# One FFN output product: steps of P2 among those of P5 and P6, Q4 in the transposes' PSUM banks, a tile of its own for the last P7, plane transfers on two steps

## The chip, the cores and the metric

The kernel runs on one core of one Trainium2 chip. The metric is the device time of one execution in microseconds (us), the median over several runs. Engine names: PE is TensorE, DVE is VectorE, ACT is ScalarE, POOL is GpSimd, SP is SyncE, which here only issues DMAs. PE sums into eight PSUM banks of 128 x 512 float32.

## What is computed

Two layers of a decoder trunk on 512 positions and 1024 channels, float32. Each layer is a half-weighted FFN, a token mixer and a second half-weighted FFN:

```python
def swiglu(x, w_in, w_out):                 # w_in 1024 x 5632, w_out 2816 x 1024
    g, u = jnp.split(x @ w_in, 2, axis=-1)
    return (jax.nn.silu(g) * u) @ w_out

for i in range(2):
    h = h + 0.5 * swiglu(rms_norm(h, ffn1_norm[i]), ffn1_w_in[i], ffn1_w_out[i])
    hn = rms_norm(h, mix_norm[i])
    m = recurrent_mixer(hn, ...) if i == 0 else spatial_gating_mixer(hn, ...)
    h = h + m
    h = h + 0.5 * swiglu(rms_norm(h, ffn2_norm[i]), ffn2_w_in[i], ffn2_w_out[i])
return rms_norm(h, final_norm)
```

So four FFNs, in the order FFN 1 and FFN 2 of layer 0, FFN 1 and FFN 2 of layer 1, with the recurrent mixer between the first two and the spatial one between the last two. The change concerns the output product, `(512 x 2816) @ (2816 x 1024)`, of the first three of them.

## The kernel before

**Number format.** Every float32 operand of a large product is split into a high part `hi` (rounded to the format that PE multiplies) and the rest `lo`; a product is three matmuls, hi·hi, lo·hi and hi·lo (L421, L422, L423). ACT writes `hi` (`act`, L103) and DVE `lo` (`tt`, L94). For the weights these are `whi` and `wlo`, made by `Sub.split`.

**Seven products.** A product of 2 x 2 blocks is done with seven products instead of eight (the form of Winograd). On the left stand blocks of the activations and sums of them, on the right blocks of the weights and sums of them:

```python
LEFT = {"P1": "A11", "P2": "A12", "P5": "S1", "P6": "S2", "P3": "S4", "P7": "S3", "Q4": "A22"}
```

The weight sums are made in SBUF. One raw tile (`Raw`, 128 x 1024 float32, 512 KB) holds two K blocks of 128 rows and 512 columns. SP loads it (`Raw.fetch`, L142). A further block is added to it in place by an accumulating DMA that POOL issues (`Raw.add`, L145), or DVE adds another tile to it (`Sub.add`, L94). For a cut i of the K dimension the weights go from product to product, in `seven` with `chain`:

- P1 and P2 load their own block.
- P5i loads the block (0,0) and gets (0,1) by an accumulating DMA, two steps after the load (`wait=2`).
- P6i takes P5i's tile; DVE adds the tile (1,1) to it. Right behind P6i's split POOL issues the addition of (1,0): that makes Q4i's weights.
- P3i loads (1,1). Right behind its split POOL issues the addition of (0,1): that makes P7i's weights. So P7i's tile is there only when P3i is split and the transfer that follows has landed.

**One output product per FFN.** In three FFNs (`FF_WHOLE`, `CHAIN`) the whole K of 22 blocks, 11 per half, is done in one pass: `out_blocks` calls `seven` with six cuts, cut 0 of one K block, the others of two. A step is one product over one cut, six matmuls per K block (12 in most steps). There are 7 x 6 = 42 steps, in the order that `CHAIN` spells out by hand: six of P1, six of P2, then a middle in which P5, P6 and four of Q4 alternate, then a tail with P3, P7 and the last two of Q4. The fourth FFN goes in three passes and doesn't use `CHAIN`.

**What sets the order.** The program is written out step by step into one queue per engine (the loop at the end of `trunk`): in step i the pending additions go to POOL, the hooks "pre" are run, weights are split up to `SPLIT_AHEAD = 3` steps ahead, the hooks "mid" and "rest" are run, further raw tiles are loaded while fewer than `RAW_BUFS = 8` are in use, the matmuls of step i follow, then the hooks "end" and "late". Nothing is reordered after that; each engine works through its queue and waits where data are missing. There are four buffers each for `whi` and `wlo`.

**PSUM.** Six banks in `mmp` (`bank`), two in `auxp` (`aux`). In the output product P1 sums into two banks A, P2 into B, P5 into C, and Q4, whose sums are kept apart here (`apart`), into two banks Q. P6 and later P7 continue in A, P3 in C:

```python
BANK = {"P1": ("A", True), "P2": ("B", True), "P5": ("C", True), "P6": ("A", False), "P3": ("C", False),
        "P7": ("A", False), "Q4": ("A", False)}
```

**What follows each product.** Behind the last step of P2, P3, P7 and Q4 DVE adds the sums to the quarters of the residual `X` (`upd`, L100): A11, A12, A22, A21. As each quarter is finished (`norm.quarter`) the next norm takes it up: squares on ACT, then transposes on PE by which the next block gets its left operands. Two of the norms do that in blocks (`BlockNorm`; transposes in `Group.turn`, L274, tile `e`; the splits behind them in tiles `hi` and `lo`). The first FFN's norm (`TileNorm`) scales whole rows first (`rows`, tile `xn`) and transposes these in two halves of sixteen (`turn`, L615, tile `xt`). The first two of four banks of a half are from `aux`.

**The left operands of a chained FFN** come from the input half of the FFN, in chunks of four columns of tiles (`chunk`, `left_blocks`). `Group.cross` transposes them by DMA: `move` copies the float32 halves apart into planes (tile `pl`, ACT) and issues two transposing DMAs on SP for each of two names (L320), all in one step; `merge` puts them together five and six steps later.

**Neighbours on the queues.** In the output product of the first FFN the gate weights of the recurrent mixer are fetched from step 8 on (`load_gates`: POOL clears a tile, L1105, then SP loads it, L1109, eight loads in all). In that of the third FFN ACT issues four DMAs of the spatial mixer in step 34 (`prep_ws`, L1287 and L1291). The first raw tiles of the stage behind (for an FFN, by `PairRaw`, L936) are loaded as slots come free in the tail.

Of the kernel before, what the change touches and what calls it, by code (L numbers as in the profile page):

```python
# [14 lines left out]
P = 128  # L15
# [34 lines left out]
CHAIN = ([("P1", i) for i in range(6)] + [("P2", i) for i in range(6)]  # L50
# [9 lines left out]
def trunk(ctx: ExitStack, tc: tile.TileContext, a: dict, out: bass.AP):  # L60
# [194 lines left out]
    class Group:  # L255
# [48 lines left out]
        def cross(self, half, tiles, planes, merges, parts):  # L304

            w, names = 2 * self.n * P, ("A12", "A11") if half == 0 else ("S1", "A22")
            if half == 0:
                names = names[::-1]
            dt = {}

            def move():
                pl = [sp.tile([P, 2 * T], U16, tag="s", name=nm("pl"))[:, : 2 * w] for _ in tiles]
                for k, name in enumerate(names):
                    c = slice(k * w, (k + 1) * w)
                    d = dt[name] = sp.tile([P, 2 * T], U16, tag="s", name=nm("dt"))[:, : 2 * w]
                    v = d.rearrange("p (m s t) -> p m s t", s=2, t=P)
                    for s, (t, h) in enumerate(zip(pl, tiles)):
                        act(t[:, c].rearrange("p (b f) -> p b f", b=2),
                            h.bitcast(U16)[:, c].rearrange("p (f b) -> p b f", b=2), AF.Copy)
                        nc.sync.dma_start_transpose(out=v[:, :, s, :], in_=t[:, c])  # L320
                tiles.clear()

            def merge(name):
                act(self.new(name).bitcast(U16).rearrange("p (x b) -> p x b", b=2),
                    dt.pop(name).rearrange("p (b x) -> p x b", b=2), AF.Copy)

            hook(*planes, move)
            for name, at in zip(names, merges):
                hook(*at, lambda name=name: merge(name))
            for name, at in zip(names, parts):  # L330
                hook(*at, lambda name=name: self.parts(name))
# [42 lines left out]
    def seven(block, cuts, left, w, posts, order=None, own=False, apart=False, joined=None, opening=None,  # L374
# [14 lines left out]
        def mm_of(prod, ci):  # L389
# [3 lines left out]
            def mm(sub):  # L393
                if fresh and ci == 0:
                    for s in range(2):
                        bk[name, s] = bank(name)[:, :w]
                if prod == joined and ci == 0:
                    held.extend((sub, q, i) for q, i in enumerate(pairs))
                    return
                if opening and prod == "P1":  # L400
                    qs = list(enumerate(pairs))
                    for n, (q, i, m, s) in enumerate([(q, i, m, s) for q, i in qs for m in range(3) for s in range(2)]
                                                     if ci == 0 else
                                                     [(q, i, m, s) for m in range(3) for q, i in qs for s in range(2)]):
                        if n == (4 if ci else 6):
                            opening[ci]()
                        nc.tensor.matmul(bk[name, s], left(prod, i, s)[m == 1], (sub.lo if m == 2 else sub.hi)[:, q, :],
                                         start=(i, m) == (0, 0), stop=(i, m) == (cuts[-1][-1], 2))
                    for s in range(2 * ci):
                        posts[prod](s, bk[name, s])  # L410
                    return
                for s in range(2):
                    ps = bk[name, s]
                    k = {} if fresh else dict(skip_group_check=True)
                    if prod == joined and also is not None:
                        also(s, ps)
                    for sb, q, i in (held if prod == joined else []) + [(sub, q, i) for q, i in enumerate(pairs)]:
                        zh, zl = left(prod, i, s)
                        wh, wl = sb.hi[:, q, :], sb.lo[:, q, :]
                        end = i == cuts[-1][-1]  # L420
                        nc.tensor.matmul(ps, zh, wh, start=fresh and i == 0, stop=False, **k)  # L421
                        nc.tensor.matmul(ps, zl, wh, start=False, stop=False, **k)  # L422
                        nc.tensor.matmul(ps, zh, wl, start=False, stop=end, **k)  # L423
                    if ci == len(cuts) - 1 and prod in posts:
                        posts[prod](s, ps)
# [4 lines left out]
        def far(ci):  # L430
            return own and order.index(("P6", ci)) - order.index(("P5", ci)) >= 4

        def again(ci):
            return own and order.index(("P5", ci)) - order.index(("P1", ci)) >= 6

        for prod, ci in order:
# [8 lines left out]
            if chain:  # L445
# [4 lines left out]
                elif prod == "P6":  # L450
                    r, tile, then = raw[11, ci], new(1, 1), block(1, 0, cuts[ci])
                elif prod == "P3":
                    r, then = new(1, 1), block(0, 1, cuts[ci])
                    raw[33, ci] = r
                else:
                    r = raw[33 if prod == "P7" else 11, ci]
            elif prod == "P1":
# [82 lines left out]
    class BlockNorm:  # L540


        def __init__(self, grow, plain=False, late=False, wait=()):


            self.g = [Group(2), Group(2)]
            self.grow, self.plain, self.late, self.wait = grow, plain, late, wait

        def src(self, i, name):
# [4 lines left out]
        def quarter(self, name):  # L554
# [5 lines left out]
            at = n + (2 if name == "A11" or name in self.wait else 1)  # L560
            for i, g in enumerate(self.g):
                g.stage(at, name, *self.src(i, name), self.plain if name == "A21" else name != "A22",
                        bank if self.late and name == "A11" else None,
                        direct=int(name == "A21" and not self.plain), lag=i)
            if name == "A21":
                S.z = self.g
# [22 lines left out]
    class TileNorm:  # L589
# [14 lines left out]
                    else:  # L604
                        ts(o, xt(t, c), S.rt[:, t : t + 1], None, ALU.mult)

        def turn(self):
            self.ps = []
            for j in range(4):
                ps = (aux if j < 2 else bank)("xt")  # L610
                for q in range(2):
                    c, k = divmod(2 * j + q, 4)
                    for s in range(2):
# [16 lines left out]
        def quarter(self, name):  # L630
# [18 lines left out]

# [1049 lines left out]
```

## Time and profile before

| | |
|---|---|
| runs | 1600.75, 1605.91, 1604.55 us; median 1604.55 |
| profiled execution | 1606.85 us, its span in the trace 1605.0 |
| granted PE clock, mean | 0.992 |
| PE busy, first output product (225.86 to 344.91) | 112.92 of 119.05 us |
| PE busy, second (700.87 to 815.79) | 110.47 of 114.92 us |
| PE busy, third (1029.98 to 1144.13) | 110.81 of 114.15 us |
| PE busy, rest of the kernel up to 1144.13 | without a gap |
| DVE busy in the three | 102.84, 98.50, 98.85 us |

The times in the second column count from the start of the span. A busy time says how long an engine had an instruction at work; a busy PE can still be slow, when its granted clock is below 1.00. In a row of instructions the releaser behind `<-` is what the engine waited for last, with the time of idleness before it.

### The profile page before, as it was taken

To read this page: it belongs to the slowest core of one execution; us is meant where nothing else is said; L and a number is where in the kernel's file an instruction comes from. 1 tells how busy PE (TensorE), PEld (TensorE's weight loads), DVE (VectorE), ACT (ScalarE), POOL (GpSimd) and SP (SyncE) were. 2 spreads that over 40 slices of the span, in tenths; PEclk is the share of its full clock that TensorE was granted. 3 is DMA by queue.
4 is the path that set the end of the run, shared out by engine and by line. 5 is a ranking of instruction groups with operands and counts; after the bars stand their busy time and mean duration, and the time that the engine had idled before them with its cause. 6 is when DMAs were issued, how large, how long until landed. Compare 5 with 4: busy or idle time off the path is not lost.

```text
span 1605.0 us, 20741 instructions
## 1 busy us (share of the span) xinstructions
PE 1581.6 (99%) x7149; PEld 1304.4 (81%) x7149; DVE 1315.6 (82%) x1759; ACT 1158.9 (72%) x1696; POOL 222.5 (14%) x201
## 2 busy tenths in 40 slices
PE   9999999999999999999899999999999999999998
PEld 7788887788888888888788888887788888888886
DVE  6977777978998877778878777789878989889788
ACT  7877786558777777786567777865786775675676
POOL 2111103200010111102201111022211011111120
PEclk9999999999999999999999999999999999999999
DMA  8888779953283887779937888799888557796793
GB/s 292 182 189 192 186 213 245 202 138 97 87 213 103 178 205 193 182 222 240 209 99 182 190 193 186 211 253 200 218 199 209 158 124 194 181 221 172 174 225 100
DMA packets 247465, 299.24 MB, mean 186 GB/s; under 512 B 94672, under 2 KB 120384, under 8 KB 247360
## 3 DMA queue, kind: packets, MB, share of 16 engines
q1 hardware_dynamic: 197856, 204.78, 41.4%
q0 software_dynamic: 47712, 91.30, 33.9%
q10 hardware_dynamic: 1792, 1.84, 0.3%
q8 instruction: 56, 0.92, 0.2%
q14 instruction: 49, 0.40, 0.1%
HBM read 275.84 MB, written 2.10 MB: 173 GB/s over the span
## 4 chain that ended last, share of the span: by engine, by line
PE 79%; DMA 6%; issue 5%; DVE 4%; ACT 2%; POOL 1%; ACTq 0%; SPq 0%; POOLq 0%
PE A L421 12%; PE A L422 12%; PE A L423 12%; PE C L422 6%; PE C L423 6%; PE C L421 6%; DMA raw<-in_ffn_w_out_dram 6%; PE p L892 4%; PE B L421 3%; PE B L423 3%; PE B L422 3%; PE r L232 2%; PE r L234 2%; PE r L233 2%; PE e L274 1%
## 5 line engine op out<-in xcount | busy, mean ns | idle before, releaser
L94 DVE TENSOR_TENSOR wlo<-raw,whi 128x1024 fp32r<-128x1024 f32 (+1 forms) x537 | 639.0, 1192 | 230.6 <-ACT whi L103 228.6
L103 ACT ACTIVATE whi<-raw 128x1024 fp32r<-128x1024 f32 (+1 forms) x537 | 553.1, 1031 | 237.5 <-PE C L422 58.4
L421 PE MATMUL A<-whi,hi 128*128 128x512 f32 x1016 | 401.0, 395 | 1.9 <-ACT c L103 1.9
L422 PE MATMUL A<-whi,lo 128*128 128x512 f32 x1016 | 396.9, 391 | 0.0
L423 PE MATMUL A<-wlo,hi 128*128 128x512 f32 x1016 | 396.9, 391 | 0.0
L421 PEld LDWEIGHTS A<-whi,hi 128*128 128x128 f32 x1016 | 191.9, 189 | 46.7 <-ACT c L103 7.9
L423 PEld LDWEIGHTS A<-wlo,hi 128*128 128x128 f32 x1016 | 191.4, 188 | 40.6 <-DVE wlo L94 0.4
L422 PEld LDWEIGHTS A<-whi,lo 128*128 128x128 f32 x1016 | 191.8, 189 | 39.0 <-DVE lo L94 0.3
L422 PE MATMUL C<-whi,lo 128*128 128x512 f32 x560 | 218.9, 391 | 1.3 <-DVE lo L94 1.2
L421 PE MATMUL C<-whi,hi 128*128 128x512 f32 x560 | 218.2, 390 | 0.0
L423 PE MATMUL C<-wlo,hi 128*128 128x512 f32 x560 | 218.1, 389 | 0.0
L145 POOL DMA_DIRECT2D raw<-in_ffn_w_in_dram x82 | 99.1, 1215 | 731.4 <-ACT pl L103 312.2
L103 ACT ACTIVATE hi<-a 128x512 fp32r<-128x512 f32 (+1 forms) x188 | 111.6, 600 | 55.9 <-DVE a L94 54.3
L145 POOL DMA_DIRECT2D raw<-in_ffn_w_out_dram x72 | 83.3, 1196 | 367.4 <-DVE wlo L94 185.6
L94 DVE TENSOR_TENSOR raw<-raw,raw 128x1024 f32<-128x1024 f32 (+1 forms) x108 | 129.6, 1200 | 0.9
L422 PEld LDWEIGHTS C<-whi,lo 128*128 128x128 f32 x560 | 105.1, 188 | 25.8 <-DVE lo L94 4.1
L421 PEld LDWEIGHTS C<-whi,hi 128*128 128x128 f32 x560 | 105.2, 188 | 21.9
L94 DVE TENSOR_TENSOR lo<-a,hi 128x512 fp32r<-128x512 f32 (+1 forms) x188 | 122.0, 656 | 1.3 <-ACT hi L103 1.2
L423 PEld LDWEIGHTS C<-wlo,hi 128*128 128x128 f32 x560 | 105.1, 188 | 21.6
L422 PE MATMUL B<-whi,lo 128*128 128x512 f32 x280 | 109.1, 389 | 0.1
L421 PE MATMUL B<-whi,hi 128*128 128x512 f32 x280 | 109.0, 389 | 0.0
L423 PE MATMUL B<-wlo,hi 128*128 128x512 f32 x280 | 109.0, 389 | 0.0
(184 smaller groups left out, 2081.3 us busy)
## 6 DMA issues: line engine op xcount, KB each, us to landing
raw<-in_ffn_w_in_dram SPq DMA_DIRECT2D x161, 512.0 KB, 4.3
raw<-in_ffn_w_out_dram SPq DMA_DIRECT2D x100, 512.0 KB, 5.6
raw<-in_ffn_w_in_dram POOLq DMA_DIRECT2D x82, 512.0 KB, 7.0
raw<-in_ffn_w_out_dram POOLq DMA_DIRECT2D x60, 512.0 KB, 7.5
raw<-in_sg_w_in_dram SPq DMA_DIRECT2D x20, 512.0 KB, 6.2
raw<-in_ffn_w_in_dram SPq DMA_DIRECT2D x34, 256.0 KB, 6.5
raw<-in_rec_w_in_dram SPq DMA_DIRECT2D x16, 512.0 KB, 3.7
raw<-in_sg_w_in_dram POOLq DMA_DIRECT2D x12, 512.0 KB, 7.7
```

What stands on the lines that cost most here:

```text
L94: nc.vector.tensor_tensor(out=o, in0=x, in1=y, op=op)
L103: nc.scalar.activation(out=o, in_=x, func=f, **k)
L145: nc.gpsimd.dma_start(out=self.v, in_=src, accum_op=ALU.add)
L232: nc.tensor.matmul(ps, wh, xh, start=start, stop=False)
L233: nc.tensor.matmul(ps, wh, xl, start=False, stop=False)
L234: nc.tensor.matmul(ps, wl, xh, start=False, stop=stop)
L274: nc.tensor.transpose(ps[:, o : o + P], src(q, s), ident)
L421: nc.tensor.matmul(ps, zh, wh, start=fresh and i == 0, stop=False, **k)
L422: nc.tensor.matmul(ps, zl, wh, start=False, stop=False, **k)
L423: nc.tensor.matmul(ps, zh, wl, start=False, stop=end, **k)
L892: nc.tensor.matmul(bank_of(half, s), z, (sub.lo if m == 2 else sub.hi)[:, q, :], start=left[2] == "2" and (h, q, m) == (0, 0, 0), stop=lef ...
```

## The change

It is confined to the three chained output products and to the chunks in front of them.

- `CHAIN`: P1 stays first. P2, which followed it in six steps, is put among the steps of P5, P6 and Q4, with P20 behind P50 and P25 next to the end of the middle. The tail is the same as before, from P30 to Q45.
- Banks: the two Q banks are taken from `aux` in a chained product. The norm behind it (`norm.chain`) takes banks from `mmp` for its transposes, except those of A21. For `TileNorm` the first half takes all four banks from `mmp`, the second as before two of each.
- P75: a product P7 that stands fewer than four steps behind P3 of its cut (`linked`) doesn't continue P3's tile but gets a tile of its own, block (0,1) loaded by SP and (1,1) added by POOL two steps later. In `CHAIN` that is P75 alone; P35 then has no addition behind its split. One 512 KB load more per chained FFN, as many additions as before.
- `Group.cross`: `move` is called once for each of the two names, on two successive steps; the merges stay where they were.

```diff
-CHAIN = ([("P1", i) for i in range(6)] + [("P2", i) for i in range(6)]
-         + [("P5", 0), ("P5", 1), ("P6", 0), ("P5", 2), ("P6", 1), ("P5", 3), ("P6", 2), ("Q4", 0), ("Q4", 1),
-            ("P5", 4), ("P6", 3), ("Q4", 2), ("P5", 5), ("P6", 4), ("Q4", 3), ("P6", 5)]
-         + [("P3", 0), ("P3", 1), ("P3", 2), ("P3", 3), ("P7", 0), ("P7", 1), ("P3", 4), ("P7", 2), ("P3", 5),
-            ("P7", 3), ("P7", 4), ("P7", 5), ("Q4", 4), ("Q4", 5)])
+CHAIN = [("P1", i) for i in range(6)]
+CHAIN += [(s[:2], int(s[2])) for s in
+          "P50 P20 P51 P60 P21 P52 P61 P22 P53 P62 Q40 P23 P54 P63 Q41 P24 P55 P64 Q42 P25 P65 Q43".split()]
+CHAIN += [(s[:2], int(s[2])) for s in "P30 P31 P32 P33 P70 P71 P34 P72 P35 P73 P74 P75 Q44 Q45".split()]
...
-            def move():
-                pl = [sp.tile([P, 2 * T], U16, tag="s", name=nm("pl"))[:, : 2 * w] for _ in tiles]
-                for k, name in enumerate(names):
-                    c = slice(k * w, (k + 1) * w)
...
-                tiles.clear()
+            def move(k, name):
+                if k == 0:
+                    dt["pl"] = [sp.tile([P, 2 * T], U16, tag="s", name=nm("pl"))[:, : 2 * w] for _ in tiles]
+                c = slice(k * w, (k + 1) * w)
...
-            hook(*planes, move)
+            for k, name in enumerate(names):
+                hook(planes[0] + k, planes[1], lambda k=k, name=name: move(k, name))
...
-                        bk[name, s] = bank(name)[:, :w]
+                        bk[name, s] = (aux if chain and name == "Q" else bank)(name)[:, :w]
...
+        def linked(ci):
+            return order.index(("P7", ci)) - order.index(("P3", ci)) >= 4
+
...
                 elif prod == "P3":
-                    r, then = new(1, 1), block(0, 1, cuts[ci])
-                    raw[33, ci] = r
+                    r = raw[33, ci] = new(1, 1)
+                    if linked(ci):
+                        then = block(0, 1, cuts[ci])
+                elif prod == "P7" and not linked(ci):
+                    r = new(0, 1, (1, 1))
                 else:
                     r = raw[33 if prod == "P7" else 11, ci]
...
-                        bank if self.late and name == "A11" else None,
+                        bank if (self.late and name == "A11") or (self.chain and name != "A21") else None,
...
-        def turn(self):
+        def turn(self, half):
             self.ps = []
             for j in range(4):
-                ps = (aux if j < 2 else bank)("xt")
+                ps = (aux if j < 2 and half else bank)("xt")
...
-                hook(n + 2, "end", self.turn)
+                hook(n + 2, "end", lambda: self.turn(0))
...
-                hook(n + 3, "end", self.turn)
+                hook(n + 3, "end", lambda: self.turn(1))
...
-        chain = not hasattr(norm, "last")
+        chain = norm.chain = not hasattr(norm, "last")
```

More of the change, by code (lines that the diff above doesn't have):

```diff
@@ L309, in cross @@
             dt = {}
-            def move():
-                pl = [sp.tile([P, 2 * T], U16, tag="s", name=nm("pl"))[:, : 2 * w] for _ in tiles]
-                for k, name in enumerate(names):
-                    c = slice(k * w, (k + 1) * w)
[L315 to L320, printed above, removed]
-                tiles.clear()
+            def move(k, name):
+                if k == 0:
+                    dt["pl"] = [sp.tile([P, 2 * T], U16, tag="s", name=nm("pl"))[:, : 2 * w] for _ in tiles]
+                c = slice(k * w, (k + 1) * w)
+                d = dt[name] = sp.tile([P, 2 * T], U16, tag="s", name=nm("dt"))[:, : 2 * w]
+                v = d.rearrange("p (m s t) -> p m s t", s=2, t=P)
+                for s, (t, h) in enumerate(zip(dt["pl"], tiles)):
+                    act(t[:, c].rearrange("p (b f) -> p b f", b=2),
+                        h.bitcast(U16)[:, c].rearrange("p (f b) -> p b f", b=2), AF.Copy)
+                    nc.sync.dma_start_transpose(out=v[:, :, s, :], in_=t[:, c])
             def merge(name):
@@ L546, in __init__ @@
             self.g = [Group(2), Group(2)]
+            self.chain = False
             self.grow, self.plain, self.late, self.wait = grow, plain, late, wait
```

## The prediction

> **What bounds the kernel now.** I read the page first, then the busy time by stretches, cut at step boundaries of the three output products that the change touches, then the waits of TensorE (PE), and last the chain of waits around each.
>
> ```profile
> span 1605.0 us, 20741 instructions
> PE 1581.6 (99%) x7149; PEld 1304.4 (81%) x7149; DVE 1315.6 (82%) x1759; ACT 1158.9 (72%) x1696; POOL 222.5 (14%) x201
> ```
>
> PE is the bound: 23.4 us of the span are all that it ever idles. A gain can come only out of that and out of stretches in which it runs slowly. Stretches (start and end, length, busy time and count of each engine, granted clock, DMA share, GB/s), one P1+P2 run, then three middles (P50 to the first P3 step), then three tails (to the end of Q45):
>
> ```profile
> 700.87:730.79 29.92, 29.92 (x133) 24.78 (x132) 24.34 (x35) 23.55 (x33) 4.51 (x4) 1.00 0.90 246
> 255.78:300.20 44.42, 42.13 (x175) 33.51 (x174) 37.75 (x50) 26.48 (x40) 10.88 (x12) 0.96 0.93 220
> 730.79:771.78 40.99, 40.78 (x183) 33.34 (x182) 37.43 (x48) 27.05 (x41) 10.30 (x10) 1.00 0.96 229
> 1059.90:1102.06 42.16, 41.15 (x183) 33.26 (x182) 36.79 (x49) 25.66 (x40) 10.71 (x10) 1.00 0.92 219
> 300.20:344.91 44.71, 40.87 (x174) 33.28 (x173) 41.40 (x66) 28.96 (x48) 6.49 (x6) 0.92 0.83 186
> 771.78:815.79 44.01, 39.76 (x173) 32.61 (x172) 36.73 (x49) 27.16 (x45) 6.02 (x5) 0.92 0.78 186
> 1102.06:1144.13 42.07, 39.74 (x173) 31.97 (x172) 38.52 (x50) 28.43 (x46) 10.22 (x10) 0.96 0.98 228
> ```
>
> and, from the timeline, eight transposes of the normalisation:
>
> ```profile
> 734.87 1.04 PE L274 MATMUL e<-ident,x 128*128 128x128 f32 x8
> ```
>
> P1+P2 has 132 product matmuls in 29.92 us: 0.2267 us each, and a two-block step of 12 takes 2.72. A middle has 29 K blocks of six matmuls, 174 x 0.2267 = 39.4; the second and third also hold eight transposes (1.0, last row). A tail has 26 blocks, 35.4, and sixteen transposes, 2.1. So the three middles are 5.0, 0.5 and 1.7 us too long and the three tails 7.2, 6.5 and 4.6: 25.5 us in all, the most that this change can win. Who waits in them:
>
> ```profile
> PE e L274 <- DVE x L100: 6.3, 3, 4.1
> PE xt L615 <- ACT xn L103: 3.2, 1, 3.2
> PE Q L421 <- ACT whi L103: 1.3, 1, 1.3
> ```
>
> and the longest of these in the timeline:
>
> ```profile
> 796.04 0.39 PE L423 MATMUL A<-wlo,hi 128*128 128x512 f32 x1
> 800.55 2.35 PE L274 MATMUL e<-ident,x 128*128 128x128 f32 x8 [4.12 <-DVE x L100]
> 803.12 0.63 PE L422 MATMUL A<-whi,lo 128*128 128x512 f32 x1
> 803.55 0.63 PE L423 MATMUL A<-wlo,hi 128*128 128x512 f32 x1
> ```
>
> An idle stretch is paid twice: after the 4.12 us the matmuls start 0.43 us apart (803.12, 803.55) instead of 0.2267, and the first two tails have a granted clock of 0.92. "TensorE: Matmul & The Clock Gate" in the Trainium skill (Why this matters for your kernels) says that only gaps over about 3 us do this; by that rule the 1.3 us wait in the first middle should have left the clock alone, and that middle has 0.96, so I let the row decide.
>
> **The last P7 on its own tile.** P75's weights are P35's tile plus an accumulating transfer that GpSimd (POOL) can issue only when P35 is split. The chain of waits before the 4.12 us:
>
> ```profile
> 788.53 8.34 DMA raw<-in_ffn_w_out_dram
> 796.97 1.06 ACT whi L103
> 798.06 0.56 DVE wlo L94
> ...
> 799.89 0.22 DVE x L100
> ```
>
> and the rows that P74's tile hangs on: its split on ACT, its add on POOL, the load for which the slot of P70 was used, and the median landings of SP's and POOL's transfers:
>
> ```profile
> 790.01 1.04 ACT L103 ACTIVATE whi<-raw 128x1024 fp32r<-128x1024 f32 x1
> 783.85 1.20 POOL L145 DMA_DIRECT2D raw<-in_ffn_w_out_dram  x1 [4.99 <-DVE wlo L94]
> 778.92 0.92 SPq L936 DMA_DIRECT2D raw<-in_ffn_w_in_dram  x2
> raw<-in_ffn_w_out_dram SPq DMA_DIRECT2D x100, 512.0 KB, 5.6
> raw<-in_ffn_w_out_dram POOLq DMA_DIRECT2D x60, 512.0 KB, 7.5
> ```
>
> The split waits for the transfer, and the update of x behind it, on which the transposes wait, stands in VectorE's (DVE) queue behind that split. In the changed program P75 has a tile loaded when P70 is split, with its add two steps later: the 8.34 us are gone from this chain. What is late next is P74. Its add (783.85) now stands on POOL behind P75's add, which waits for its load: that load takes the slot freed at 778.92, lands 5.6 later at 784.5, POOL needs 1.2, so P74's add goes out at 785.7, 1.9 us later, and lands by the median 7.5 at 793.2. P74's split began at 790.01: it would be 1.9 us late (if the add lands as fast as it must have) to 4.0 us (by the 8.34). Against this, that split could have begun when PE ended P34, at 788.1 (771.78 + 2 x 1.36 + 5 x 2.72), and was 1.9 us late for a backlog on DVE that the middle leaves (next part). P75's round from split to x takes 4.1 us (796.97 to about 801.1), P74's before it one step, 2.7: without any wait x would be there some 7 us after 790.0, at 797, and PE is ready for it at 796.3 (796.04 + 0.2267). With the backlog gone and P74 0 to 4.0 late on that, the idle time is 0 to 2.9 us instead of 4.12; I take 1.5, and 0.6 at half rate. The second FFN, with a tail 6.5 too long, saves 4.4.
>
> In the first FFN the normalisation of rows follows, and its root stands behind the same split:
>
> ```profile
> 319.48 7.76 DMA raw<-in_ffn_w_out_dram
> 327.34 1.07 ACT whi L103
> ...
> 332.06 1.97 PE xt L615 x8
> ```
>
> The split that waits 7.76 us for its tile ends at 328.4, and from there to the transposes are 3.6 us. The update of x is in place before it here, so without that wait the 3.2 us of PE idle shrink by 0 to 2.8, by how late P74 is; I take 2, and 1.0 of matmuls at half rate: 3.0. In the third the chain is another:
>
> ```profile
> 1122.53 1.22 ACTq L1291
> 1123.87 1.07 ACT whi L103
> 1128.70 1.29 DVE x L100 x2
> ```
>
> ScalarE (ACT) issues four DMAs of the next mixer from step P34 on, the split comes after them, x after that. The change leaves them where they are. I give it 1.0 (0 to 2, or up to 2 worse if P74 is late on top).
>
> Cost of the tile: three more 512 KB loads on SyncE's (SP) queue, and the next stage's first loads one slot later. At 246 GB/s (first stretch row) that is 2.1 us each; the steps that need the delayed tiles come eight and more steps later, so I cost it at nothing; uncovered it is 2.1 us in each.
>
> **P2 over the middle.** The same steps in another order, no matmul more. What it does to supply:
>
> ```profile
> 273.79 2.00 ACT L103 ACTIVATE whi<-raw 128x1024 fp32r<-128x1024 f32 x2 [3.54 <-DMA raw<-in_ffn_w_out_dram]
> 272.97 2.44 POOL L145 DMA_DIRECT2D raw<-in_ffn_w_out_dram  x2 [9.36 <-DMA raw<-in_ffn_w_out_dram]
> SPq L1109 <- POOL gw L1105: 8.0, 1, 8.0
> 261.89 10.52 DMA raw<-in_ffn_w_out_dram
> 1066.67 9.64 DMA raw<-in_ffn_w_out_dram
> L94 DVE TENSOR_TENSOR wlo<-raw,whi 128x1024 fp32r<-128x1024 f32 (+1 forms) x537 | 639.0, 1192 | 230.6 <-ACT whi L103 228.6
> ```
>
> All middle stalls end in a split of Q4 or P3 whose add is not there. The add for Q4 goes out when P6 is split. Before, it is needed four or five steps later (Q41: P51, P60, P52, P61, which are 9.5 us, against 9.64 in the last row). In the new order seven to nine steps lie between, for Q40 the shortest, 15.0 us. In the first FFN SP also stands still: eight gate loads wait 8.0 us for POOL's memsets, and these for the adds ahead of them (POOL waited 9.36 us for a load later on), while the weight load at the end of it lands after 10.52. In the new order two adds fewer stand ahead of the memsets, so part of this goes. DVE is busy 91% of a middle (37.43 of 40.99) and 81% of P1+P2 (24.34 of 29.92); with P2's half mixed in it comes to 49.6 of 55.9, 89%. Over the whole second product it is busy 98.5 us (the three rows) of the 107.9 that PE needs without a wait, so it is no bound of its own, but makes up a hole only over many steps. I keep 1 us of stall in the first FFN and 0.7 in the others together: of 7.2 us 5.5 are saved. What moves the other way: the x update of P2, the squares and the transposes of A11 now come after P25, at the start of the tail. That is some 2.6 us of DVE (two updates, 1.29 in the row above, and two lo like them) in a tail where it is busy 36.73 of some 37.5 us net, part of that the backlog. Splits run three steps, 8.2 us, ahead of PE, so it is covered; if the backlog stays, it costs up to 2.6 in each of two FFNs. I take 1.4 for all new costs (0 to 6).
>
> **Q4 in the transposes' banks; two plane transfers a step.** Q keeps the two spare banks from Q40 to the end, and the transposes take banks that B and C have left two or more steps earlier (B at P25, C at P35); for the first FFN four banks are needed after P74, and exactly four are free. Nothing waits. The plane transfers are split over two steps, their merges stay; the chunk stages around them run without a gap (P1+P2 row: busy 29.92 of 29.92), so there is nothing to win and five steps of cover to lose. Both zero, the second within 1 us.
>
> **Sum.** 4.4 + 3.0 + 1.0 + 5.5 - 1.4 = 12.5. The profiled execution took 1606.85 us around its span of 1605.0; the median of the runs is 1604.55, 0.14% less, which changes a saving of 12.5 us by nothing. 1604.55 - 12.5 = 1592.0. With the bounds: 20 us if P74 is on time and the middle clean, 6 if its wait is at its worst.
>
> **Rivals.**
> 1. *P74 takes over P75's wait whole.* Its add lands at 794 and the DVE backlog is not smaller. Tails stay (-1), the middle saves 5.5: 1599. For: POOL's order is in the program. Against: both adds were needed before too, and P75's leaves the end of the queue.
> 2. *The DMA engines are the limit and only move the waits.* The middles run at DMA share 0.92 to 0.96, and every byte still has to come, plus 1.5 MB. "DMA: Bandwidth & Descriptors" in the Trainium skill (Issuing engines are not separate DMA queues) speaks for this: all issuers share the same 16 engines. Gains of 6 against losses of 6: 1604. Against: PE needs a block per 1.36 us in either order, and the first stretch row carried 246 GB/s where the middles carried 219 to 229.
> 3. *Slower: P53 comes late.* Its tile is a load in step P14 and an add on top in step P50, two transfers in series. From P14 to P53's own start are 23.1 us (25.8 in the old order), less 2.3 for the split that frees the slot (1.1 on ACT, then 1.2 on DVE, last row above) and 2.3 for its own: 18.5. By the medians the pair takes 13.1; by the worst rows above 10.5 + 9.6 + 1.2 = 21.3, which is 3 us of idle and some 2 at half rate. In three FFNs 15 us, the middle's gain gone, the tails' 7.4 kept: 1612. It decides once the pair exceeds 18.5.
>
> **Numbers.** About 0.3%, 4.8 us, is what a measurement of this kernel can tell from no change. Chances: forecast 0.62 (its own range 1584 to 1599), rival 1 0.14, rival 2 0.12, rival 3 0.12. Faster by over 0.3% (below 1599.7) is the forecast and most of rival 1: 0.73; same, the rest and rival 2: 0.14; slower 0.13. The range goes from 1583 to 1603: below are the cleanest tails, above rival 3 and half of rival 2.
>
> **What would show it.** Right: middles of about 40 us without ACT waits on DMA before Q4 splits; a second tail of about 40 with a transposes' wait under 3 us; the third tail still waiting on ACT's DMA issues; granted clock near 1.0 in the middles. Wrong: a wait of ACT on P74's tile as long as the old one; waits of ACT in steps P52 to P55; PE waiting for a PSUM bank; a PE gap in a chunk stage.

## The result: 0.8% slower

| | us, median | range | runs |
|---|---|---|---|
| before | 1604.55 | 1600.75 to 1606.44 | 7 |
| changed | 1614.54 | 1610.57 to 1625.56 | 7 |

The ratio is 1.0077, 95% interval 1.0048 to 1.0106: 8 to 17 us slower, where 12 us faster was forecast. The changed kernel's profile is of the shortest of its seven runs (1610.57), that of before of a long one (1606.85, above all seven in the table); the spans differ by 3.8 us only. So the profiles show what kinds of stall there are, and the sizes come from the medians.

The page, and the stretches as cut before (three middles, from P50 to the first P3 step, then three tails):

```profile
span 1608.8 us, 20740 instructions
PE 1579.2 (98%) x7149; PEld 1302.5 (81%) x7149; DVE 1315.1 (82%) x1759; ACT 1156.6 (72%) x1696; POOL 223.1 (14%) x201
```

```profile
239.67:297.35 57.68, 55.62 (x241) 44.67 (x240) 49.62 (x65) 33.60 (x48) 13.46 (x14) 1.00 0.96 235
713.45:769.71 56.26, 55.50 (x249) 45.72 (x248) 48.35 (x63) 32.81 (x48) 11.96 (x11) 1.00 0.96 233
1044.53:1101.08 56.55, 55.71 (x250) 45.73 (x248) 48.58 (x63) 33.16 (x48) 12.20 (x11) 1.00 0.96 238
297.35:342.45 45.10, 40.42 (x173) 31.99 (x172) 39.78 (x65) 30.27 (x52) 6.05 (x5) 0.96 0.82 189
769.71:815.35 45.64, 40.64 (x175) 32.95 (x174) 37.56 (x50) 30.40 (x51) 5.59 (x5) 0.93 0.79 189
1101.08:1147.87 46.79, 39.12 (x175) 32.05 (x174) 37.66 (x50) 30.06 (x51) 10.28 (x10) 0.93 0.88 215
```

A middle now holds 40 K blocks (P5, P2, P6 and four of Q4), 240 x 0.2267 = 54.4 us. Less that, and less 1.04 for transposes in the second and third, the middles are 3.3, 0.8 and 1.1 us too long (before 5.0, 0.5, 1.7). The tails, less 35.4 and 2.1, are 7.6, 8.1 and 9.3 too long (before 7.2, 6.5, 4.6). The middles gave 2 us, the tails took 6.7; the rest of the 3.8 us is that the first output product begins 1 us earlier. What TensorE (PE) waits for:

```profile
PE e L273 <- DVE x L99: 12.4, 2, 7.5
PE C L421 <- DVE lo L93: 3.4, 5, 0.8
PE xt L621 <- ACT xn L102: 3.2, 1, 3.2
```

The wait for the update of x doubled (6.3 before) and the one before the row norm stands where it stood. The chain of waits in the second tail:

```profile
777.75 4.71 DMA raw<-in_ffn_w_out_dram
...
783.05 0.71 POOL raw L144
783.75 9.87 DMA raw<-in_ffn_w_out_dram
...
793.73 1.07 ACT whi L102
...
797.25 0.74 DVE wlo L93
...
798.99 0.49 DVE x L99
```

and GpSimd's (POOL's) instructions there:

```profile
783.02 2.44 POOL L144 DMA_DIRECT2D raw<-in_ffn_w_out_dram  x2 [6.69 <-DVE wlo L93]
```

and P74's split on ScalarE (ACT):

```profile
793.73 1.06 ACT L102 ACTIVATE whi<-raw 128x1024 fp32r<-128x1024 f32 x1 [4.43 <-DMA raw<-in_ffn_w_out_dram]
```

From top to bottom: P75's own load lands at 782.5 (POOL's row names DVE, but the load ended later), POOL issues P75's addition and 0.7 us behind it P74's, and P74's takes 9.87 us, to 793.6. Its split starts at 793.7, 24.0 us into the tail; before, it started at 790.0, 18.2 us into a tail that began 2.1 us later. Then P75's split still stands ahead of x.

### The profile page after: what moved, and what is told of

It reads as the page before. It is cut to its first block, busy times and chain, and to the rows that moved or that the text cites. A ratio compares the mean times of both kernels' runs of the same rounds, so it can differ in the third digit from the quotient of the medians.

```text
span 1608.8 us, 20740 instructions
## 1 busy us (share of the span) xinstructions
PE 1579.2 (98%) x7149; PEld 1302.5 (81%) x7149; DVE 1315.1 (82%) x1759; ACT 1156.6 (72%) x1696; POOL 223.1 (14%) x201
## 4 chain that ended last, share of the span: by engine, by line
PE 82%; DMA 7%; DVE 5%; ACT 1%; issue 1%; POOL 0%; POOLq 0%; ACTq 0%; DVEq 0%
PE A L420 13%; PE A L421 13%; PE A L422 13%; DMA raw<-in_ffn_w_out_dram 7%; PE C L421 6%; PE C L422 6%; PE C L420 6%; PE p L898 4%; PE B L422 3%; PE B L421 3%; PE B L420 3%; PE r L231 2%; PE r L232 2%; PE r L233 2%; DVE wlo L93 2%; PE e L273 1%
```

## The experiments

Times are against the kernel before, run on the same chip in the same rounds (its medians there 1603.3 to 1604.4); us are the ratio's, with the 95% interval. Each kernel ran 5 to 12 times. The groups e, f, g, h and j ran on five chips, so kernels of different groups are compared by their ratios. The profile of each kernel is of one execution, in e1 and h1 of a long one (1618.7 and 1611.4 us).

| run | what it is | ratio | us |
|---|---|---|---|
| e0_again | changed kernel | 1.0085 | +13.6 (10.4 to 16.8) |
| e1_no_tile | P75 on P35's tile | 1.0016 | +2.6 (0.2 to 5.0) |
| e2_add_after | P75's addition behind P74's | 1.0006 | +1.0 (-1.9 to 3.9) |
| e3_old_move | transfers in one step | 1.0046 | +7.4 (4.7 to 10.1) |
| f1_order_alone | order and banks alone | 1.0001 | +0.2 (-2.1 to 2.4) |
| f3_tile_alone | own tile alone | 1.0104 | +16.7 (14.0 to 19.2) |
| h2_tile_add_after | own tile alone, addition last | 1.0002 | +0.3 (-1.9 to 2.7) |
| f4_move_alone | transfers on two steps alone | 1.0011 | +1.8 (-0.6 to 4.2) |
| f2_repaired | order, tile with addition last, one step | 0.9980 | -3.2 (-4.8 to -1.8) |
| g1_x_first | f2 and two queue edits | 0.9950 | -8.0 (-10.9 to -5.0) |
| g2_x_first_no_tile | g1, P75 on P35's tile | 0.9971 | -4.7 (-6.6 to -2.7) |
| g3_p2_earlier | f2, P20 to P22 ahead of P50 | 0.9999 | -0.2 (-2.2 to 2.1) |
| h1_p25_earlier | f1, P25 three steps earlier | 1.0022 | +3.5 (1.0 to 5.9) |
| h3_root_first | g1, root ahead of P75's split | 0.9949 | -8.2 (-10.9 to -5.3) |
| h4_old_order | g1 with the old order | 0.9968 | -5.1 (-7.5 to -2.9) |
| j1_move_again | g1, transfers on two steps | 0.9985 | -2.4 (-4.5 to -0.3) |
| j2_merges_later | j1, merges a step later | 0.9975 | -4.0 (-5.9 to -1.9) |

### Where the loss is: one part undone at a time

The changed kernel itself:

> The changed kernel once more, as the yardstick for the other three. Its seven runs spread from 1610.6 to 1625.6 us, its profile is of the shortest of them. Theory T (tail): the loss is in the tails, where P74's tile comes late; a second profile has the three waits of TensorE before the normalisation's transposes at 3 to 10 us again, and 10 to 17 us for the whole run over the kernel before. Theory M (middle): the loss is in the middles, in steps of P5 whose additions come late; a second profile that is longer than the first by 4 us or more has them there. Theory B (bytes): 1.5 MB more in a busy time; both, in like parts.

It gave 1617.4 us and the same picture (waits of 7.1, 5.2 and 3.2 us before the transposes). Then without the tile (`linked` always true):

```diff
-            return order.index(("P7", ci)) - order.index(("P3", ci)) >= 4
+            return True
```

> The changed kernel, with P75 on P35's tile again (no load more, the addition behind P35's split as in the kernel before). Theory T: the tails go back to what they were, 0.4, 1.6 and 4.7 us less than in the changed kernel's profile, so about 1607, within 3 us of before. Theory M: no gain, 1612 to 1616, and the waits in P52 and P54 stay. Theory B: some 3 us back (a third of the loss), 1611.

1606.2 us, 11 less than the changed kernel: theory T. Then all parts kept, but P75's addition one step later:

```diff
-                    r = new(0, 1, (1, 1))
+                    r = new(0, 1, (1, 1), 3)
```

> The changed kernel, with the addition to P75's own tile one step later, so that GpSimd issues P74's addition ahead of it; all bytes are the same. Theory T, in the form that the order of the two additions on GpSimd's queue is what makes P74 late (the two land some 5 us behind each other): P74 lands about 5 us earlier, P75 then is the last but has its time, the three tails lose 3 to 5 us each, 1601 to 1605. Theory B: the pair of additions ends when it did, and the splits with it, 1613 to 1616. Theory M: tails as T says or not, the waits in the middle stay, and the time stays above the kernel before by 3 us or more.

1606.0 us: the same bytes in another order on one queue, and 11 us less. That decides against theory B. In its second tail P74's addition goes out at 779.40 and lands in 5.86 us, and its split starts 19.6 us into the tail; P75's addition is now the second and the slow one:

```profile
779.40 0.47 POOL raw L144
779.87 0.50 issue
780.37 10.19 DMA raw<-in_ffn_w_out_dram
```

The total came out 1 to 5 us above what T gave, so something else may have been costing as well. The same kernel as the changed one, with the transfers in one step:

```diff
-                hook(planes[0] + k, planes[1], lambda k=k, name=name: move(k, name))
+                hook(planes[0], planes[1], lambda k=k, name=name: move(k, name))
```

> The changed kernel, with all four plane transfers of a group issued in one step again, as before. Theory M in the form that the loads of P5 and P2 are held on SyncE's queue behind the second pair of transposing transfers, which wait for ScalarE's copies up to 3.9 us: the waits in P52 of 1.1 us go, and P53 to P55 with them, 2 to 5 us in all, 1610 to 1612. Theories T and B: no change, within 2 us of the changed kernel.

1610.5 us, 6 to 7 less than the changed kernel, as theory M in this form had it, but not by its mechanism: the wait in P52 stayed (1.3, 1.2 and 0.9 us in the three middles). What went is a wait in another place, below.

### The tile is GpSimd's queue

```diff
+        def linked(ci):
+            return order.index(("P7", ci)) - order.index(("P3", ci)) >= 4
...
-                    r, then = new(1, 1), block(0, 1, cuts[ci])
-                    raw[33, ci] = r
+                    r = raw[33, ci] = new(1, 1)
+                    if linked(ci):
+                        then = block(0, 1, cuts[ci])
+                elif prod == "P7" and not linked(ci):
+                    r = new(0, 1, (1, 1))
```

on the kernel before, nothing else:

> The kernel before with P75's own tile alone, as the change has it (addition two steps behind the load, ahead of P74's). Theory S: 8 to 12 us slower than before, 1612 to 1616, with P74's addition landing 9 to 12 us after its issue in the tails. If the tile only costs where the new order has left a backlog of VectorE in the tail: within 4 us of before.

1621.2 us, more than the whole change cost. POOL in the second tail, the chain there, and PE's waits over the kernel:

```profile
791.94 2.44 POOL L145 DMA_DIRECT2D raw<-in_ffn_w_out_dram  x2 [8.72 <-DVE a L94]
```

```profile
783.29 8.09 DMA raw<-in_ffn_w_out_dram
...
792.67 10.71 DMA raw<-in_ffn_w_out_dram
...
810.00 1.12 PE e L274 x4
```

```profile
PE e L274 <- DVE x L100: 17.8, 2, 9.2
PE A L421 <- ACT whi L103: 4.6, 1, 4.6
```

POOL stands 8.7 us, by the chain until P75's load lands, which takes 8.1 us; then both additions go out 0.7 us apart and the second, P74's, lands 10.7 us later, at 803.4. The parts don't add up: the tile cost 16.7 alone, on the new order 7 (1.0046 against 1.0001) or 11 (e0 against e1). That P75's load took only 4.7 us in the changed kernel fits this; it was not tried by itself.

The same with the addition a step later, `new(0, 1, (1, 1), 3)`:

> The kernel before with P75's own tile alone, its addition one step later, behind P74's on GpSimd's queue. If the 17 us that the tile alone cost come from that place in the queue: 1601 to 1605, level with before. If they come from the load more or from the later addition in the old order's tail: 1610 or more.

1605.0 us, level with before. P74's addition goes out alone and P75's after it:

```profile
784.82 1.20 POOL L145 DMA_DIRECT2D raw<-in_ffn_w_out_dram  x1 [4.75 <-DVE wlo L94]
787.00 1.20 POOL L145 DMA_DIRECT2D raw<-in_ffn_w_out_dram  x1 [0.97 <-DMA raw<-in_ffn_w_out_dram]
```

So the 16.7 us are the place of one addition in POOL's queue, and the load more costs nothing measurable.

### The two plane transfers

`move` of the change on the kernel before, `hook(planes[0] + k, ...)`:

> The kernel before with the plane transfers on two steps alone. Theory S: 5 to 8 us slower, 1609 to 1612, with transposing transfers that land 10 to 16 us after their issue (9 at most before) and waits of ScalarE for them in the chunk stages (none before). If those waits come only with the new order's traffic: within 2 us of before.

1606.3 us, +1.8 with an interval that holds zero, so not the 5 to 8 of theory S. What sets it apart is the transposing transfers' time from issue to landing (first row: before, second: f4), and ACT's wait for them in the merges, which the kernel before does not have:

```profile
DMA to landing us min/median/max: 2.3/2.5/9.0
```

```profile
DMA to landing us min/median/max: 2.3/3.7/14.8
```

```profile
ACT a L103 <- DMA dt<-pl: 9.3, 6, 4.6
```

In the list of ACT's waits no kernel with the transfers on one step has it (twelve kernels, thirteen profiles, median landings 2.4 to 3.2 us); all seven profiles with two steps (six kernels) do (8.7 to 17.8 us, median landings 3.7 to 4.1). And the time goes outside the middles and tails: less what these are too long, the spans of the thirteen profiles are 1579 to 1581 us, those of the seven 1578 to 1594, six of them over 1583. The profile of e1:

```profile
212.24 1.18 ACT L102 ACTIVATE a<-dt 128x1024 uint16<-128x1024 uint16 x1 [6.94 <-DMA dt<-pl]
```

ACT stands 6.9 us with all splits behind it in its queue, and PE 3.5 us at 224.5. What gets in between can be seen on SyncE (SP), before and then in the changed kernel:

```profile
190.38 7.05 SPq L320 DMA_TRANSPOSE dt<-pl  x4
```

```profile
189.23 2.50 SPq L319 DMA_TRANSPOSE dt<-pl  x2
191.82 0.53 SPq L141 DMA_DIRECT2D raw<-in_ffn_w_out_dram  x1
192.79 4.28 SPq L319 DMA_TRANSPOSE dt<-pl  x2
```

so a load now goes out between the pairs, and so do POOL's additions: in one chunk they are issued at 549.3 and 551.6, and the second pair, issued at 551.6 and 553.4, takes 13.4 and 12.2 us; before, they came at 551.8 and 554.0, and the pair's first at 553.0 took 7.3. That these in front are the cause was not tried by itself. To measure this where the tails are quiet, the same line on the fastest version (g1, below):

> The fastest version (new order, P75's tile with its addition last, the two edits of the queues; 1595.7, ratio 0.9950) with the plane transfers on two steps put back, as in the change. So far that split has cost 1.8, 2.4, 4.2 and 6.3 us in four pairs. Theory D (transposing transfers that are issued after other transfers of the next step land 10 to 16 us later, and ScalarE stands still for them in the merge, with the splits queued behind it): 1598 to 1601, with waits of ScalarE for these transfers and a spread of 8 us or more. If the cost was only that of its meeting the stalled tails: 1594 to 1597.

1601.8 against 1595.7 us: 5.6 us, with intervals that don't touch (0.9972 to 0.9998 against 0.9932 to 0.9969), runs from 1596 to 1607, and ACT waiting 15.4 us for them. Then with later merges:

```diff
-            g.cross(half, hs, (n, "mid"), ((n + 5, "mid"), (n + 6, "mid")), ())
+            m = n + (5 if g.tail else 6)
+            g.cross(half, hs, (n, "mid"), ((m, "mid"), (m + 1, "mid")), ())
...
+                    groups[-1].tail = j == len(sizes) - 1
```

> The same with the two merges one step later, so seven and eight steps' hooks instead of six and seven, in all chunks but the last of each FFN, which has no room for it. Theory D: 2.7 us more of cover in four of five chunks, most of the waits of ScalarE for these transfers go, 1595 to 1598. If the transfers hurt in another way (loads and additions behind them): 1598 to 1601, the same as without.

1599.6 us, between the two, with overlapping intervals, and ACT still waits 13.1 us (four times in place of eight, 6.3 the longest). A step of cover more is not enough for transfers that late; whether they hurt in another way too stays open.

### The order of P2

Alone, that is the changed kernel with `linked` true and one step for the transfers:

> The new order of P2 with its banks alone: the changed kernel with P75 on P35's tile and all plane transfers in one step, both as before. Theory S (the loss is the sum of two separate costs, the own tile 10 to 11 us and the two transfers' steps 6 to 7, and the order brings a small gain): 13.6 less 10.5 less 6.5, so 3 to 4 us faster than before, 1600 to 1602. Theory O (the order itself brings what the prediction gave it, 4 to 6, and the parts make each other worse): 1598 to 1600. Theory M (the middle loses by it): 1606 or more.

1604.0 us: neither S nor O, no gain that can be measured. Its middles are better by the profile (3.3, 0.8 and 0.3 us too long), and what is left there is mostly P52's wait (1.2, 0.9 and 0.5 us; in the first middle also 1.3 at P54). In the second middle of the changed kernel the chain before P52 is an addition:

```profile
711.10 9.95 DMA raw<-in_ffn_w_out_dram
...
721.15 1.07 ACT whi L102
...
724.13 0.50 PE C L421
```

Two other orders:

```diff
-          "P50 P20 P51 P60 P21 P52 P61 P22 P53 P62 Q40 P23 P54 P63 Q41 P24 P55 P64 Q42 P25 P65 Q43".split()]
+          "P20 P21 P22 P50 P51 P60 P52 P61 P53 P62 Q40 P23 P54 P63 Q41 P24 P55 P64 Q42 P25 P65 Q43".split()]
```

> The repaired version with P20, P21 and P22 ahead of P50 again and the rest of P2 spread as in the change. Theory L (the order's gain is eaten by P52 and P54, whose load and addition in series have only the P1 run to arrive in, while SyncE stands behind the transposing transfers at the start of it): the waits in P21 and P52, 1.7, 1.8 and 0.7 us in the three middles, go and nothing comes for them, 3 to 4 us, 1597 to 1598. If what the order brings at Q4 is lost again by this: 1601 to 1604.

1604.2 us, 3 more than f2 by the ratios, with intervals that overlap slightly, and P52 still waits (2.6, 1.2 and 1.3 us): theory L is wrong.

```diff
+          "P50 P20 P51 P60 P21 P52 P61 P22 P53 P62 P23 Q40 P54 P24 P63 Q41 P25 P55 P64 Q42 P65 Q43".split()]
```

> The new order alone (P75 on P35's tile, transfers in one step), with P22 to P25 packed closer so that P25 ends three steps earlier and the work on the first quarter of x (update, squares, transposes, their splits) falls into the middle again. Theory G (the order gives back in the tail what it wins in the middle, because that work now stands on VectorE's queue at the start of the tail: waits in P32, P71 and P34 of 2.0, 0.4 and 0.2 us): these go, 1601 to 1602 against 1604 for the order alone. Theory L2 (the gain is eaten by P52 and P54 alone): no change, 1603 to 1605.

1606.4 us. By the profile the tail's waits at P71 and P34 went, but others came: 2.1 us at P24 in the first middle (row below), and in the second and third product steps 1.8 us too long at P64 and 1.0 each at P31 and P32. No evidence for G in this form.

```profile
PE B L421 <- DVE lo L93: 2.1, 1, 2.1
```

A second look at the kernel before:

> The kernel before once more, for a second profile of its tails, since single executions of one program spread by 6 to 9 us. If the tails are a fixed cost: three tails 7, 6 and 5 us too long again, within 1 us each. If they hang on how the transfers happen to land: one of them differs by 2 us or more from the first profile.

1601.6 us, with middles 7.7, 1.0 and 2.3 us too long and tails 3.8, 2.3 and 3.5. So a tail differs by up to 4 us between two executions of one program; the 25.5 us of the prediction were those of one long execution, and this one had 20.6.

### Together

Order, tile with its addition last, transfers in one step:

> The new order, P75's own tile with its addition behind P74's on GpSimd's queue, and all plane transfers in one step. Theory S: like the order alone, 1598 to 1602, since an own tile whose addition stands last took as long as P35's tile did (1606.0 against 1606.2). If the own tile is worth what one profile shows (5 us less in the first tail): 1595 to 1597.

1601.2 us, clear of the kernel before. What is still waited for there is x behind P75's split in the second tail, and ACT's DMA issues in the third. Two edits to the queues: the first puts the update of x ahead of P75's split in the second FFN too, the second lets ACT issue the spatial mixer's four DMAs three steps later.

```diff
-        if isinstance(norm, TileNorm) or getattr(norm, "late", False) or getattr(norm, "plain", False):
+        if chain or isinstance(norm, TileNorm) or getattr(norm, "late", False) or getattr(norm, "plain", False):
...
-        hook(at0 - 8, "late", prep_ws)
+        hook(at0 - 5, "late", prep_ws)
```

> The repaired version (new order, P75's tile with its addition last, transfers in one step) with two edits to what waits in line: in the second FFN the update of x stands ahead of P75's split on VectorE's queue, as it does already in the first and third, and in the third FFN ScalarE issues the four DMAs of the spatial mixer three steps later, behind P75's split. Theory Q (what stalls the tails is work in line behind a split that waits for its addition, or behind DMA issues on ScalarE, not the supply as such): the waits of 3.2 and 2.6 us before the transposes in the second and third tail go with their half-rate matmuls, 6 to 8 us, 1593 to 1596. Theory B (the bytes come no sooner): the waits turn up at P75's or P74's matmuls, 0 to 2 us, 1599 to 1602.

1595.7 us. Its tails, and PE's waits:

```profile
297.16:338.55 41.39, 38.41 (x173) 30.62 (x172) 38.20 (x62) 29.16 (x51) 6.05 (x5) 1.00 0.86 196
766.37:805.51 39.14, 38.27 (x175) 30.88 (x173) 36.89 (x50) 30.11 (x53) 5.57 (x5) 1.00 0.87 216
1091.12:1131.78 40.66, 38.16 (x175) 30.96 (x174) 37.21 (x49) 29.50 (x52) 8.89 (x9) 1.00 0.94 233
```

```profile
PE e L273 <- DVE x L99: 3.4, 6, 1.4
PE C L421 <- DVE lo L93: 2.8, 4, 0.8
PE xt L621 <- ACT xn L102: 2.1, 1, 2.1
```

The second tail is 1.6 us too long where the changed kernel's was 8.1, at a granted clock of 1.00: theory Q. Without the tile:

> The same two edits on the new order alone, where P75 continues P35's tile. Theory Q: the same 6 to 8 us, 1596 to 1598, and it stays 0 to 3 us behind the version with the tile, since P75's addition is issued later there. Theory B: 1602 to 1605.

1598.6 us, 3 more, intervals that overlap slightly. With the root of the first FFN's row norm ahead of P75's split (the late split left out for `TileNorm`):

> The fastest version so far (1595.7) with one edit more: in the first FFN the root of the row norm stands ahead of P75's split on VectorE's and ScalarE's queues. Theory Q: the wait of 2.1 us before the sixteen transposes loses 1.1 to 2 us, with what follows at half rate 1 to 3 us in all, 1593 to 1595. If that wait is the backlog ahead of the update of x instead: 1595 to 1597, no change.

1595.6 us, no change, though the wait before those transposes fell from 2.1 to 1.25 us. With `CHAIN` as before on the fastest version:

> The fastest version so far with the old order of P2 (six steps behind P1) put back, all else as there. Theory G (with the tails cleared, the order's gain in the middle shows: about 8 us of stalls in the three old middles by the mean of four profiles, 5 in the new ones): 1598 to 1600, 3 us slower than with the new order. If the order is worth nothing even so: 1594 to 1597. If the own tile with its addition last needs the new order's slots: 1602 or more.

1599.1 us: the order is worth 3 us there. Its interval overlaps that of the new order slightly; the other such pair, h2 and f2 (P75's addition last, without the queue edits), gives 3.5 us with intervals 0.9988 to 1.0017 and 0.9970 to 0.9989.

## Why the prediction was wrong, point by point

**"The last P7 on its own tile", 8.4 us saved (4.4 + 3.0 + 1.0).** This step failed, with its sign: 16.7 us lost alone, 7 to 11 on the new order. That P75's addition stands ahead of P74's was seen, and so was the delay of P74's issue by 1.9 us (783.75 against 783.85 before, by a program that was 2.1 us earlier there). Mis-sized was how late P74 is. The prediction let its split start 1.9 to 4.0 us late, from landings of up to 8.34 us, and took 1.9 off again for "a backlog on DVE that the middle leaves".

Measured, the split started 5.8 us late (24.0 against 18.2 us into the tail): the addition took 9.87 us, in the third tail 11.7, on the old order 10.7. Two additions issued 0.7 us apart do not land side by side; the second came 4 to 6 us after the first in the six tails of the changed kernel and f3. The next stage's loads were in flight beside them (L942, from 785.1 in the second tail), and their share isn't separated; but with the two additions swapped and all bytes kept (e2) it is P75's that takes 10.19 us, and the loss is gone.

PE's idle time before the transposes was 4.9 us, where 1.5 was taken and 2.9 was the worst; in the third tail it was 7.5, and in the first the 3.2 us stayed, of which 2 were to go. The 7 us from P74's split to x, with P75's split between them, came true (6.5). Rival 1 had this mechanism, "Its add lands at 794" (793.6, which on the clock of the kernel before would be 795.7), and priced it at one microsecond for all tails.

**The backlog on DVE.** It did not go. In the changed kernel ACT was free for P74's split only at 789.3 (793.73 less 4.43), 19.6 us into the tail, 1.4 us later than the split of before began. The transfer hid that: DVE then stood idle 3.9 us ahead of P74's split, as it had ahead of P75's before.

**"P2 over the middle", 5.5 saved.** The cause was right: by the changed kernel's profile the long steps at Q4 are gone from the middles, but for the transposes in Q43. The size was not. In six profiles with the old order the three middles are 4.6 to 10.9 us too long together (mean 8.3), in twelve with the new one 3.0 to 6.1 (mean 4.5): 3.8 us, and P52 or P53 took over part of what was left. With P75's addition last it shows in the time, 3.0 and 3.5 us; with P75 on P35's tile it measured 0.2 (-2.1 to 2.4). **What "moves the other way"**, 1.4 us, would have to be 4 there; where it goes is not settled, since the tails of single executions differ by more than that. The sign "middles of about 40 us" could not have come: with P2 in them they need 54.4.

**"Q4 in the transposes' banks; two plane transfers a step", "Both zero, the second within 1 us".** The banks: no wait of PE for a bank stands out in the changed kernel's list, as forecast; no run has them alone. The transfers cost 1.8, 2.4, 4.2, 5.6 and 6.3 us in five pairs, the first with an interval that holds zero. The step that failed is "nothing to win and five steps of cover to lose": the cover was counted in steps (13.6 us), without asking what would be issued between the pairs; the slowest transfer of each profile took 13.4 to 18.7 us, with all in one step 8.2 to 10.5. Nor were the chunk stages without a gap: the row shown was of P1 and P2, and the kernel before has a PE wait of 1.9 us for a chunk at 66.8, so the table's "without a gap" doesn't hold for its first 225.86 us.

**The third tail: "I give it 1.0 (0 to 2, or up to 2 worse if P74 is late on top)".** By the profile it was 4.7 worse: P74's addition came later than ACT's DMA issues and hid them. They stayed, in e2 as part of the chain, and moving them is one of the two edits behind g1's gain.

**Rival 2**, that bytes only move the waits, fell: with all of the 1.5 MB more, g1 is 8 us faster. **Rival 3** had the place (P5's tile, a load and an addition in series) but not the size: in the changed kernel P52 or P53 was 1.1 to 1.3 us too long in each middle, not 5, and the step was mostly P52, not P53. The loss came from the two places that had no rival or one of one microsecond. Of the four signs named for being wrong three came: ACT waiting for P74's tile (4.43 us, for P75's 4.54 before), ACT waiting in P52 to P55 (3.0 us for P52's tile in the second middle, 4.5 for P53's in the third), and a gap of PE in a chunk stage (3.5 us in e1; in the changed kernel's own profile only 1.1).

## What to carry to other kernels

A transfer that is issued from a queue in program order belongs at the place of its need: an addition that waits for its own load, put ahead of one that is needed sooner, cost 17 us in three places, and the same one behind it nothing. Before moving an issue to another step, list what will then be issued in front of it and between its parts, and take for its landing the time when two of them go out together, not the median. And where single executions spread by 6 us, take the sizes from medians of several runs and the kinds of wait from the profile.

## What the runs showed of the hardware

- Two accumulating transfers of 512 KB that POOL issues 0.7 us apart land one after the other: 5.65 and 9.87 us after their issue in the changed kernel, 7.5 and 10.7 in f3. "DMA: Bandwidth & Descriptors" in the Trainium skill (Issuing engines are not separate DMA queues) says that all issuers share the same 16 engines; that is a rule across issuers, and these rows are of one; they show that its two transfers land 4 to 6 us apart and not together.
- The time at half rate after a wait does not follow the wait's length. In the third tail of the changed kernel 7.5 us of idle time were followed by 3.4 us of it: eight transposes 0.21 us apart (0.11 at full rate), then matmuls 0.43, 0.43 and 0.38 us apart by the chain. In the second tail 4.9 us were followed by 6.2 (eight transposes and nine matmuls), in the first middle of the kernel before 1.27 us by 3.3 (seven spacings of 0.43), and 3.0 us in its second profile by none.

```profile
1134.02 1.76 PE e L273 x7
1135.78 0.43 PE A L420
1136.20 0.43 PE A L421
1136.63 0.38 PE A L422
1137.01 0.23 PE A L420
```

"TensorE: Matmul & The Clock Gate" in the Trainium skill (Part 1: The HAM clock gate, What's actually happening) calls the window in which the chip watches TensorE free-running. That fits this scatter; the prediction's "An idle stretch is paid twice" doesn't.
